# S5 coefficient generators on VectorE alone, in smaller steps, beside the first feed-forward layer

## The chip, the core and the metric

The kernel runs on one core of a Trainium2 chip. Five engines work side by side, each through its own instruction queue: TensorE (PE in the profile, with its weight loads shown as PEld), VectorE (DVE), ScalarE (ACT), GpSimd (POOL) and SyncE (SP), which here only issues transfers. ScalarE and GpSimd issue transfers too; the profile shows their issue slots as ACTq and POOLq. An instruction that waits holds up what stands behind it in its engine's queue. The metric is device time in microseconds (us), the median over several executions.

## The reference, cut to what matters

Two layers run over 1024 latent tokens and, in the first layer, 256 context tokens, with 1024 channels. Layer 0 mixes tokens by attention and retention, layer 1 by an S5 state-space scan in both directions; after each mixer comes a squared-ReLU feed-forward product ("MLP"). The change touches the preparation of the S5 scan's coefficients, which depends on parameters alone, and the place of some adaptive-modulation work in layer 1:

```
def s5_discretize(a_re, a_im, b_re, b_im, c_re, c_im, log_dt):
    a = lax.complex(f(a_re), f(a_im))
    dt = jnp.exp(f(log_dt))[:, None]
    a_bar = jnp.exp(dt * a)
    b_bar = ((a_bar - 1) / a)[..., None] * lax.complex(f(b_re), f(b_im))
    c_mat = lax.complex(f(c_re), f(c_im))
...
for l in range(DEPTH):
    mod_l = (silu(c) @ ada_w[l] + ada_b[l])       # six vectors of 1024
    h_l = modulate(rmsnorm(x, norm1_g[l]), mod_l[0], mod_l[1])
    o_l = mixer(h_l)                              # l = 0: attention and retention; l = 1: S5
    x = x + mod_l[2] * o_l
    h_l = modulate(rmsnorm(x, norm2_g[l]), mod_l[3], mod_l[4])
    x = x + mod_l[5] * (square(relu(h_l @ w1)) @ w2)
```

In layer 1 the mixer's output goes through a gated product: `z = gelu(y) @ w_glu`, then `za * sigmoid(zb)`.

## The kernel before

Every large product is done in three passes (`mm3`, lines 70 to 72): both operands are split into a high and a low part, and high-high, high-low and low-high are summed. For a weight tile `mraw` that SP has loaded, ScalarE makes the high part (`uh` or `dh`, line 76) and VectorE the low part (`ul` or `dl`, line 84). For the activations of the MLP's middle, ScalarE makes `r` (line 1053), `ah` (1056) and the square (1057), and GpSimd makes `al` (line 84). VectorE adds each finished bank of the second product to `x` (line 1070).

The first layer's MLP runs twice: first over 512 latent and 256 context tokens ("the first pass"), then over the other 512 latent tokens ("the second pass"). Each pass has 16 groups; a group does two blocks of the first product (`first`) and then the eight output tiles of the second product for the group before (`second`). In the first pass, from group 14 on, another generator (`last`, the normalisation of the second pass's tokens) takes the place of the side work.

Beside these passes runs one chain of Python generators, the side work: the modulation sums for layer 1 (`ada_rest`, tile `aw`, line 216), then the S5 generators in the order `s5_base`, `s5_outputs`, `s5_inputs`, `s5_tables`, and last the normalisation of two token blocks (`s5_in`, tile `us`). `beat` advances the chain by one step ("tick") each time a counter of matmul work, multiplied by a rate, passes one: a unit is one 512-column matmul, and the rate is `RA` = 0.07 in the first pass and `RB` = 0.125 in the second. `later(n, f)` emits f n ticks later. What the generators do:

- `s5_base` (lines 1144 to 1307): discretises and raises a_bar to powers 0 to 8 (`pw`) on 128x64 tiles, then makes `pb` (power times the factor (a_bar-1)/a, complex, for two directions) and `bb` (that factor times b). The real and imaginary parts of a complex product need two products and a sum each. One product of each pair is made by VectorE (lines 1271, 1298) and one by GpSimd (1272, 1299); VectorE sums them a tick later (1275, 1276, 1302, 1303). Twenty ticks after `pb`, TensorE transposes it and it is stored as `pbd`.
- `s5_outputs` (lines 1377 to 1420): 16 steps of two directions. In each, GpSimd makes four products of 128x288 elements (1402 to 1405, tile `oc`), VectorE joins them two ticks later (1408, 1409), ScalarE's queue stores them five ticks later (1414, `cst`), and `s5_lags` runs 32 small matmuls on them six ticks later (1433).
- `s5_inputs` (lines 1342 to 1375): 16 parts. SP loads two tiles `wb` (line 1350) and two `ww` (1353) of 256 KB for each part, one part ahead. For the real and the imaginary part GpSimd makes two products of 128x512 (1368, 1370, tile `wo`), VectorE sums them two ticks later (1371), and ScalarE's queue stores the sum five ticks after the second product (1373, `bst`).
- `s5_tables` (lines 1309 to 1340): cosine and sine tables, on VectorE and ScalarE.

All short-lived tiles of 512 elements come from one set of 32 buffers (`atile`); the MLP's split activations hold 16 of them.

After the second pass the S5 scan runs (`s5_main`), then the gated product (`glu`, from line 1564), two token halves `th` of eight output tiles `oc`; its side work is the modulation for the second layer's MLP, one step after every fourth matmul group (line 1586). The program text is not the order of execution in full: each engine has a queue order that was fixed when the program was built, and the trace shows side work standing ahead of or behind its place in the text.

Of the kernel before, what the change touches and what calls it, by code (L numbers as in the profile page):

```python
# [13 lines left out]
ALU = mybir.AluOpType  # L14
# [10 lines left out]
MAGIC = 12582912.0  # L25
NW = 14
RA = 0.07
RB = 0.125
BLOCKS = ((0, 512), (512, 512), (1024, 256))


# [20 lines left out]
class Net:  # L52
# [1091 lines left out]
    def s5_base(self):  # L1144
        nc, I = self.nc, self.I
# [119 lines left out]
        for d in range(2):  # L1265
            o, w = self.atile(name="pb"), self.atile(name="pbw")
            o4, w4 = (x.rearrange("p (s r q) -> p s r q", s=8, r=2) for x in (o, w))
            e = slice(0, 8) if d == 0 else slice(7, None, -1)
            bc = lambda K: K[:, d::2].unsqueeze(1).to_broadcast([P, 8, 32])
            for r in range(2):  # L1270
                tt(o4[:, :, r], pr[:, e, d::2], bc((kr, ki)[r]), ALU.mult)
                nc.gpsimd.tensor_tensor(w4[:, :, r], pi[:, e, d::2], bc((ki, kr)[r]), ALU.mult)

            def add(o4=o4, w4=w4):
                tt(o4[:, :, 0], o4[:, :, 0], w4[:, :, 0], ALU.subtract)
                tt(o4[:, :, 1], o4[:, :, 1], w4[:, :, 1], ALU.add)
            self.later(1, add)

            def turn(d=d, o=o):
                tp = self.bank()  # L1280
                for k4 in range(4):
                    nc.tensor.transpose(tp[:, k4 * P:(k4 + 1) * P], o[:, k4 * P:(k4 + 1) * P], self.ident)
                st = self.atile(name="pbs")
                nc.scalar.activation(st, tp, AF.Copy)
                nc.sync.dma_start(bass.AP(tensor=self.pbd.tensor, offset=self.pbd.offset + d * 65536,
                                          ap=[[P, P], [16384, 4], [1, P]]), st.rearrange("j (k n) -> j k n", k=4))
            self.later(20, turn)
            yield

        for d in range(2):  # L1290
            x, o, t = ([self.atile(name=nm) for _ in range(2)] for nm in ("b", "bb", "bt"))
            self.bb += [o]
            for r in range(2):
                nc.scalar.dma_start(x[r], I["s5b"][r, :, d])
            kb = lambda K: K[:, d::2].unsqueeze(2).to_broadcast([P, 32, 16])
            g3 = lambda x: x.rearrange("p (g h) -> p g h", h=16)
            for r in range(2):
                tt(g3(o[r]), g3(x[r]), kb(kr), ALU.mult)
                nc.gpsimd.tensor_tensor(g3(t[r]), g3(x[1 - r]), kb(ki), ALU.mult)

            def add(d=d, o=o, t=t):
                tt(o[0], o[0], t[0], ALU.subtract)
                tt(o[1], o[1], t[1], ALU.add)
                for r in range(2):
                    v.tensor_copy(self.bx[:, d, r, 0:16], o[r][:, 496:512])
            self.later(1, add)
            yield

    def s5_tables(self):

# [31 lines left out]
    def s5_inputs(self):  # L1342

        nc, I = self.nc, self.I
        parts = [(d, g0) for d in range(2) for g0 in range(0, 64, 8)]

        def fetch(d, g0):
            b, w = ([self.atile(name=nm) for _ in range(2)] for nm in ("wb", "ww"))
            for r in range(2):
                nc.sync.dma_start(b[r], bass.AP(  # L1350
                    tensor=I["s5bt"].tensor, offset=I["s5bt"].offset + (d * 2 + r) * 4096 + g0 * 64,
                    ap=[[0, 8], [16384, 16], [1, 512]]))
                nc.sync.dma_start(w[r], bass.AP(
                    tensor=self.pbd.tensor, offset=self.pbd.offset + (d * 16 + r) * 4096 + g0 * 64,
                    ap=[[8192, 8], [0, 16], [1, 512]]))
            return b, w
        gpv = lambda x: x.rearrange("p (q n) -> p q n", n=P)
        nx = fetch(*parts[0])
        for _ in range(4):
            yield  # L1360
        for k, (d, g0) in enumerate(parts):
            b, w = nx
            if k + 1 < len(parts):
                nx = fetch(*parts[k + 1])
            qs = slice(g0 // 2, g0 // 2 + 4)
            for r in range(2):
                x, t = (self.atile(name="wo") for _ in range(2))
                nc.gpsimd.tensor_tensor(x, w[0], b[r], ALU.mult)
                yield
                nc.gpsimd.tensor_tensor(t, w[1], b[1 - r], ALU.mult)  # L1370
                self.later(2, lambda r=r, x=x, t=t: nc.vector.tensor_tensor(
                    x, x, t, ALU.add if r else ALU.subtract))
                self.later(5, lambda qs=qs, d=d, r=r, x=x: nc.scalar.dma_start(self.bst[:, qs, d, r], gpv(x)))
                yield
                yield

    def s5_outputs(self, gp):

        nc, I = self.nc, self.I
        v = nc.vector  # L1380
        pr, pi = self.pw
        nc.scalar.dma_start(self.dr, I["s5d"])
        nc.scalar.dma_start(self.eye, I["eye16"])
        for it in range(16):
            qs = slice(2 * it, 2 * it + 2)
            if it % 4 == 0:
                c = self.atile(name="c5")
                nc.scalar.dma_start(c, I["s5c"][:, 8 * it // 4:8 * it // 4 + 8].rearrange("p q d r h -> p (q d r h)"))
                c = c.rearrange("p (q d r h) -> p q d r h", d=2, r=2, h=16)
            o1 = {}  # L1390
            for d in range(2):
                x = [c[:, 2 * (it % 4):2 * (it % 4) + 2, d, r] for r in range(2)]

                ks = slice(0, 9) if d == 0 else slice(8, None, -1)
                k0 = 1 if d == 0 else 0
                w = [pw[:, ks, 4 * it + d:4 * it + d + 3:2].rearrange("p k q -> p q k").unsqueeze(3).to_broadcast(
                    [P, 2, 9, 16]) for pw in (pr, pi)]
                xb = [a.unsqueeze(2).to_broadcast([P, 2, 9, 16]) for a in x]
                v9 = lambda t: t[:, :288].rearrange("p (q k h) -> p q k h", q=2, k=9)
                a, b, e, f = (self.atile(name="oc") for _ in range(4))  # L1400
                gp_tt = nc.gpsimd.tensor_tensor
                gp_tt(v9(a), xb[0], w[0], ALU.mult)
                gp_tt(v9(b), xb[1], w[1], ALU.mult)
                gp_tt(v9(e), xb[0], w[1], ALU.mult)
                gp_tt(v9(f), xb[1], w[0], ALU.mult)

                def join(a=a, b=b, e=e, f=f):
                    v.tensor_tensor(a[:, :288], a[:, :288], b[:, :288], ALU.subtract)
                    v.scalar_tensor_tensor(e[:, :288], e[:, :288], -1.0, f[:, :288], op0=ALU.mult, op1=ALU.subtract)
                self.later(2, join)  # L1410

                def store(qs=qs, d=d, a=a, e=e, k0=k0):
                    for r, t in enumerate((a, e)):
                        nc.scalar.dma_start(self.cst[:, qs, d, r], t[:, :288].rearrange("p (q k) -> p q k", q=2)[
                            :, :, 16 * k0:16 * k0 + P])
                self.later(5, store)
                o1[d] = [t[:, :288].rearrange("p (q k) -> p q k", q=2) for t in (a, e)]
                yield
            self.later(6, lambda it=it, o1=o1: self.s5_lags(it, o1))
            yield  # L1420

    def s5_lags(self, it, o1):
# [141 lines left out]
    def glu(self, p, x, after, side):  # L1564
# [3 lines left out]
        for th in range(2):  # L1568
# [9 lines left out]
            for oc in range(KT):  # L1578
                b = []
                for w in (oc + KT, oc):  # L1580
                    wt = self.split(p, I["glu"][w], "u")
                    z = self.bank()
                    for kt in range(KT):
                        self.mm3(z, wt(kt), yT[kt], kt == 0, kt == KT - 1)
                        if kt % 4 == 3:
                            next(side, None)
                    b.append(z)
                sgm = p.tile([P, 512], F32, tag="r", name="sgm", bufs=2)
                nc.scalar.activation(sgm, b[0], AF.Sigmoid)
                nc.vector.scalar_tensor_tensor(sgm, b[1], self.M[:, 1, 2, oc, 0:1], sgm, op0=ALU.mult, op1=ALU.mult)  # L1590
                xs = self.xh(x, oc, th)
                nc.gpsimd.tensor_tensor(xs, xs, sgm.rearrange("p (t c) -> p t c", t=4), ALU.add)  # L1592
                if th or oc:
                    after(*((th, oc - 1) if oc else (0, KT - 1)))
# [265 lines left out]
```

## Time and profile before

| what | value |
|---|---|
| median of 3 runs | 3227.12 us (3220.26 to 3232.1) |
| profiled execution, its own time | 3215.43 us |
| its span in the trace | 3213.6 us |
| granted TensorE clock, mean | 0.967 of full |
| TensorE busy | 92% of the span |
| VectorE, ScalarE, GpSimd busy | 66%, 38%, 29% |
| bytes moved, mean rate | 324.28 MB, 101 GB/s |

Durations and windows below come from the profiled execution. Its first MLP pass runs from about 1075 to 1665 us, the second from there to about 2082 us, the S5 scan to about 2285 us, the gated product to about 2500 us, and the second layer's MLP to the end. A window row of the profile gives, for a stretch of time, each engine's busy microseconds, with the number of instructions in brackets, then the granted TensorE clock, the share of the 16 DMA engines and the rate in GB/s. A row of the groups view gives line, engine, operation, tiles, shapes and count, then the total busy time and the mean of one in ns, then the engine's idle time just before them and what ended it. A timeline row gives start, duration, engine, line, tiles, and in square brackets the idle time before it and what ended it.

### The profile page before, as it was taken

How to read it: one execution, taken by the hardware profiler on the slowest of the kernel's cores; microseconds unless marked ns; L12 is line 12 of the kernel's file. 1: busy time of each engine (PE TensorE's matmuls, PEld its weight loads, DVE VectorE, ACT ScalarE, POOL GpSimd, SP SyncE). 2: the span in 40 equal slices, each digit the busy share in tenths (PEclk: the TensorE clock that was granted, in tenths of full speed). 3: DMA queues.
4: the chain of work that ended last, by engine and by line, in shares of the span. 5: the costliest groups of instructions: out<-in, count | busy, mean ns of one | idle time of the engine just before them, and what ended most of it. 6: DMA issues, size and time to landing. Idle time of an engine off the chain costs nothing. (4 is left out here: it accounts for less than half of the span.)

```text
span 3213.6 us, 45368 instructions
## 1 busy us (share of the span) xinstructions
PE 2968.0 (92%) x16683; PEld 2436.2 (76%) x16683; DVE 2111.0 (66%) x4014; ACT 1221.5 (38%) x2493; POOL 929.7 (29%) x902
## 2 busy tenths in 40 slices
PE   5899998899999998999997999967799999999998
PEld 3777777678878787887785778756678788888887
DVE  6777777687754688556468974378865555555555
ACT  6542222666762332222233664321334322222221
POOL 3642222455540113466326110123222111111111
PEclk8999999999999999999998999979999999999999
DMA  7132222301021452245426555287742111111111
GB/s 250 69 119 84 76 79 63 84 26 25 13 85 34 136 162 89 87 120 154 131 85 206 172 163 145 85 180 196 231 139 89 56 46 53 53 46 47 46 46 66
DMA packets 259039, 324.28 MB, mean 101 GB/s; under 512 B 72336, under 2 KB 179632, under 8 KB 258816
## 3 DMA queue, kind: packets, MB, share of 16 engines
q1 hardware_dynamic: 198352, 281.03, 29.0%
q10 hardware_dynamic: 59264, 36.84, 3.7%
q0 software_dynamic: 1200, 3.51, 0.4%
q8 instruction: 131, 2.15, 0.3%
q14 instruction: 92, 0.75, 0.1%
HBM read 267.96 MB, written 53.35 MB: 100 GB/s over the span
## 5 line engine op out<-in xcount | busy, mean ns | idle before, releaser
L84 POOL TENSOR_TENSOR al<-r,ah 128x512 fp32r<-128x512 f32 (+1 forms) x160 | 204.3, 1289 | 1191.5 <-ACT r L1057 1116.7
L1070 DVE SCALAR_TENSOR_TENSOR x<-b,mods,x 128x512 f32<-128x512 f32 (+1 forms) x483 | 457.5, 967 | 101.1 <-PE b L72 95.1
L84 DVE TENSOR_TENSOR ul<-mraw,uh 128x512 fp32r<-128x512 f32 x256 | 204.6, 803 | 429.3 <-ACT uh L76 428.7
L70 PE MATMUL b<-ah,dh 128*128 128x512 f32 (+1 forms) x1088 | 416.1, 383 | 21.4 <-ACT r L1053 10.2
L71 PE MATMUL b<-al,dh 128*128 128x512 f32 (+1 forms) x1088 | 413.7, 380 | 0.7 <-POOL al L84 0.7
L72 PE MATMUL b<-ah,dl 128*128 128x512 f32 (+1 forms) x1088 | 412.7, 380 | 0.5 <-DVE dl L84 0.4
L76 ACT ACTIVATE uh<-mraw 128x512 fp32r<-128x512 f32 x256 | 160.3, 628 | 453.3 <-PE b L71 261.3
L70 PE MATMUL b<-h2h,uh 128*128 128x512 f32 (+1 forms) x768 | 280.7, 366 | 21.8 <-DVE x L1070 11.6
L72 PE MATMUL b<-h2h,ul 128*128 128x512 f32 (+1 forms) x768 | 278.9, 364 | 18.6 <-DVE ul L84 18.4
L71 PE MATMUL b<-h2l,uh 128*128 128x512 f32 (+1 forms) x768 | 277.5, 361 | 0.0
L70 PEld LDWEIGHTS b<-ah,dh 128*128 128x128 f32 x1088 | 206.7, 190 | 64.8 <-DVE x L1070 11.6
L72 PEld LDWEIGHTS b<-ah,dl 128*128 128x128 f32 x1088 | 206.5, 190 | 40.5 <-DVE dl L84 1.9
L71 PEld LDWEIGHTS b<-al,dh 128*128 128x128 f32 x1088 | 207.0, 190 | 38.1 <-POOL al L84 1.1
L76 ACT ACTIVATE dh<-mraw 128x512 fp32r<-128x512 f32 x192 | 117.5, 627 | 248.2 <-PE b L71 119.6
L84 POOL TENSOR_TENSOR pl<-pe,ph 128x512 fp32r<-128x512 f32 (+1 forms) x128 | 158.3, 1246 | 154.9 <-ACT ph L76 86.8
L70 PE MATMUL b<-h3h,uh 128*128 128x512 f32 x512 | 202.0, 395 | 0.0
L71 PE MATMUL b<-h3l,uh 128*128 128x512 f32 x512 | 200.0, 391 | 2.0 <-DVE h3l L313 1.8
L72 PE MATMUL b<-h3h,ul 128*128 128x512 f32 x512 | 200.9, 393 | 0.0
L70 PEld LDWEIGHTS b<-h2h,uh 128*128 128x128 f32 x768 | 146.6, 191 | 50.5 <-DVE x L1070 14.2
L84 DVE TENSOR_TENSOR dl<-mraw,dh 128x512 fp32r<-128x512 f32 x192 | 150.5, 794 | 48.5 <-ACT dh L76 28.9
L72 PEld LDWEIGHTS b<-h2h,ul 128*128 128x128 f32 x768 | 146.4, 191 | 47.1 <-DVE ul L84 23.7
L1053 ACT ACTIVATE r<-b 128x512 f32<-128x512 f32 (+1 forms) x160 | 87.9, 550 | 244.9 <-PE b L72 170.8
(421 smaller groups left out, 7171.3 us busy)
## 6 DMA issues: line engine op xcount, KB each, us to landing
mraw<-in_w SPq DMA_DIRECT2D x192, 512.0 KB
aw<-in_adat SPq DMA_DIRECT2D x112, 256.0 KB
mraw<-in_glu SPq DMA_DIRECT2D x32, 512.0 KB
aw<-in_adat SPq DMA_DIRECT2D x96, 128.0 KB
CS<-csd SPq DMA_DIRECT2D x32, 320.0 KB
w<-in_adaw SPq DMA_DIRECT2D x32, 256.0 KB
wraw<-in_winr SPq DMA_DIRECT2D x32, 256.0 KB
cst<-oc ACTq DMA_DIRECT2D x64, 128.0 KB
```

The lines of the kernel that those rows point to most:

```text
L70: mm(o, s[0], m[0], start=start, stop=False)
L71: mm(o, s[0], m[1], start=False, stop=False)
L72: mm(o, s[1], m[0], start=False, stop=stop)
L76: self.nc.scalar.activation(o, x, AF.Copy)
L84: e.tensor_tensor(o, x, h.bitcast(F32), ALU.subtract)
L1053: nc.scalar.activation(r[:, :n], b[:, :n], AF.Relu)
L1070: nc.vector.scalar_tensor_tensor(o, as_x(b), self.M[:, l, 5, oc, s:s + 1], xs, op0=ALU.mult, op1=ALU.add)
```

## The change

The products that GpSimd made in `s5_base`, `s5_outputs` and `s5_inputs` are made by VectorE. In each generator the order becomes product, product, sum, directly one after the other or one tick apart, where the sums were deferred with `later`; the stores and `s5_lags` follow at the same or a shorter distance. `s5_base` and `s5_outputs` get more ticks, `s5_inputs` keeps its six per part. `RB` goes from 0.125 to 0.14. In the gated product the side steps of the first output tile (`th` = 0, `oc` = 0) are left out, so the modulation starts one tile later. `s5_tables`, `s5_lags` and all MLP code stay as they are.

```
-RB = 0.125
+RB = 0.14
...
             for r in range(2):
                 tt(o4[:, :, r], pr[:, e, d::2], bc((kr, ki)[r]), ALU.mult)
-                nc.gpsimd.tensor_tensor(w4[:, :, r], pi[:, e, d::2], bc((ki, kr)[r]), ALU.mult)
-
-            def add(o4=o4, w4=w4):
-                tt(o4[:, :, 0], o4[:, :, 0], w4[:, :, 0], ALU.subtract)
-                tt(o4[:, :, 1], o4[:, :, 1], w4[:, :, 1], ALU.add)
-            self.later(1, add)
+                yield
+                tt(w4[:, :, r], pi[:, e, d::2], bc((ki, kr)[r]), ALU.mult)
+                tt(o4[:, :, r], o4[:, :, r], w4[:, :, r], (ALU.subtract, ALU.add)[r])
+                yield
...
+            yield
+            yield
             for r in range(2):
                 tt(g3(o[r]), g3(x[r]), kb(kr), ALU.mult)
-                nc.gpsimd.tensor_tensor(g3(t[r]), g3(x[1 - r]), kb(ki), ALU.mult)
-
-            def add(d=d, o=o, t=t):
-                tt(o[0], o[0], t[0], ALU.subtract)
-                tt(o[1], o[1], t[1], ALU.add)
-                for r in range(2):
-                    v.tensor_copy(self.bx[:, d, r, 0:16], o[r][:, 496:512])
-            self.later(1, add)
-            yield
+                yield
+                tt(g3(t[r]), g3(x[1 - r]), kb(ki), ALU.mult)
+                yield
+                tt(o[r], o[r], t[r], (ALU.subtract, ALU.add)[r])
+                v.tensor_copy(self.bx[:, d, r, 0:16], o[r][:, 496:512])
+                yield
...
                 x, t = (self.atile(name="wo") for _ in range(2))
-                nc.gpsimd.tensor_tensor(x, w[0], b[r], ALU.mult)
+                nc.vector.tensor_tensor(x, w[0], b[r], ALU.mult)
                 yield
-                nc.gpsimd.tensor_tensor(t, w[1], b[1 - r], ALU.mult)
-                self.later(2, lambda r=r, x=x, t=t: nc.vector.tensor_tensor(
-                    x, x, t, ALU.add if r else ALU.subtract))
-                self.later(5, lambda qs=qs, d=d, r=r, x=x: nc.scalar.dma_start(self.bst[:, qs, d, r], gpv(x)))
+                nc.vector.tensor_tensor(t, w[1], b[1 - r], ALU.mult)
                 yield
+                nc.vector.tensor_tensor(x, x, t, ALU.add if r else ALU.subtract)
+                self.later(3, lambda qs=qs, d=d, r=r, x=x: nc.scalar.dma_start(self.bst[:, qs, d, r], gpv(x)))
                 yield
...
-                gp_tt = nc.gpsimd.tensor_tensor
-                gp_tt(v9(a), xb[0], w[0], ALU.mult)
-                gp_tt(v9(b), xb[1], w[1], ALU.mult)
-                gp_tt(v9(e), xb[0], w[1], ALU.mult)
-                gp_tt(v9(f), xb[1], w[0], ALU.mult)
-
-                def join(a=a, b=b, e=e, f=f):
-                    v.tensor_tensor(a[:, :288], a[:, :288], b[:, :288], ALU.subtract)
-                    v.scalar_tensor_tensor(e[:, :288], e[:, :288], -1.0, f[:, :288], op0=ALU.mult, op1=ALU.subtract)
-                self.later(2, join)
+                v.tensor_tensor(v9(a), xb[0], w[0], ALU.mult)
+                v.tensor_tensor(v9(b), xb[1], w[1], ALU.mult)
+                v.tensor_tensor(a[:, :288], a[:, :288], b[:, :288], ALU.subtract)
+                yield
+                v.tensor_tensor(v9(e), xb[0], w[1], ALU.mult)
+                v.tensor_tensor(v9(f), xb[1], w[0], ALU.mult)
+                v.scalar_tensor_tensor(e[:, :288], e[:, :288], -1.0, f[:, :288], op0=ALU.mult, op1=ALU.subtract)
...
-                self.later(5, store)
+                self.later(3, store)
...
-            self.later(6, lambda it=it, o1=o1: self.s5_lags(it, o1))
+            self.later(4, lambda it=it, o1=o1: self.s5_lags(it, o1))
...
-                        if kt % 4 == 3:
+                        if kt % 4 == 3 and (th or oc):
                             next(side, None)
```

## The prediction, written before the changed kernel ran

> **What bounds the kernel now.** First the page's table of busy time, then the windows of the two MLP passes beside which the generators run.
>
> ```profile
> PE 2968.0 (92%) x16683; PEld 2436.2 (76%) x16683; DVE 2111.0 (66%) x4014; ACT 1221.5 (38%) x2493; POOL 929.7 (29%) x902
> ```
> ```profile
> 1200.00:1280.00 80.00, 69.21 (x382) 59.07 (x381) 72.56 (x198) 19.60 (x41) 32.44 (x33) 0.96 0.28 86
> 1280.00:1360.00 80.00, 80.00 (x561) 69.04 (x560) 39.10 (x57) 22.84 (x49) 28.93 (x35) 1.00 0.30 91
> 1360.00:1480.00 120.00, 112.76 (x879) 93.22 (x878) 69.93 (x117) 34.94 (x82) 77.54 (x97) 1.00 0.39 115
> 1480.00:1560.00 80.00, 67.60 (x407) 57.29 (x406) 44.96 (x50) 18.41 (x40) 46.71 (x34) 0.91 0.64 201
> 1560.00:1640.00 80.00, 80.00 (x463) 70.41 (x462) 34.17 (x45) 25.96 (x52) 11.22 (x11) 1.00 0.22 67
> 1640.00:1760.00 120.00, 97.31 (x441) 77.55 (x440) 93.64 (x115) 38.27 (x66) 66.94 (x45) 0.86 0.54 169
> 1760.00:1880.00 120.00, 116.94 (x504) 93.98 (x503) 116.46 (x287) 78.67 (x140) 16.41 (x12) 1.00 0.58 176
> 1880.00:1960.00 80.00, 78.03 (x344) 63.83 (x344) 44.62 (x73) 45.42 (x76) 8.61 (x7) 0.98 0.56 148
> 1960.00:2040.00 80.00, 80.00 (x349) 65.04 (x348) 31.84 (x45) 32.16 (x52) 10.20 (x8) 1.00 0.40 122
> ```
>
> TensorE bounds the kernel, and only its idle time can be won. From 1200 to 1760 us it idles 10.79 + 0 + 7.24 + 12.40 + 0 + 22.69 = 53.1 us. The idle stretches are those with high POOL time; where GpSimd does nothing for the generators (1560 to 1640), PE is full. With VectorE at 116.46 of 120 us but GpSimd quiet (the tables, 1760 to 1880), PE still loses only 3.06 us. So a loaded VectorE alone is not what hurts.
>
> A gap also costs afterwards. After a gap of 6.26 us TensorE restarts at half clock:
>
> ```profile
> 1548.80:1552.80 4.00, 3.92 (x9) 3.15 (x10) 2.01 (x3) 0.03 (x1) 0.78 (x1) 0.50 1.02 283
> 1552.80:1556.80 4.00, 4.00 (x18) 3.26 (x17) 0.00 (x0) 0.15 (x1) 0.00 (x0) 0.90 0.55 194
> ```
>
> 9 matmuls in 4 us in place of 18: 2 us lost. The PE timeline shows six such slow starts, matmuls of 0.8 us behind a gap of over 3 us; the first and the last:
>
> ```profile
> 1253.26 0.80 PE L72 MATMUL b<-h2h,ul 128*128 128x512 f32 x1 [7.53 <-DVE ul L84]
> ...
> 1746.69 0.80 PE L70 MATMUL b<-h2h,uh 128*128 128x512 f32 x1 [8.49 <-DVE x L1070]
> ```
>
> One lies before 1280 us, two in 1480 to 1560, three after 1640: 12 us by these rows. The Trainium skill ("TensorE: Matmul & The Clock Gate", the HAM clock gate) puts the slow stretch at about 3.4 us at half clock; six of these would be an estimated 10 us, and the pool would shrink by 2. By the rows the pool is 53 + 12 = **65 us**, 2% of the time.
>
> Who keeps TensorE waiting: the waits of PE in 1200 to 1760, then the groups, and a stretch of the timeline of all engines.
>
> ```profile
> PE b L72 <- DVE ul L84: 18.4, 5, 7.5
> PE b L70 <- DVE x L1070: 16.7, 7, 8.5
> PE b L70 <- ACT r L1053: 10.2, 3, 6.3
> ```
> ```profile
> L84 DVE TENSOR_TENSOR dl<-mraw,dh 128x512 fp32r<-128x512 f32 x59 | 54.6, 947 | 17.3 <-ACT dh L76 17.3
> L1371 DVE TENSOR_TENSOR wo<-wo 128x512 f32<-128x512 f32 x32 | 40.2, 1258 | 18.6 <-POOL wo L1370 17.4 <-DMA wb<-in_s5bt 1.2
> L1408 DVE TENSOR_TENSOR oc<-oc 128x288 f32<-128x288 f32 x32 | 23.7, 741 | 21.6 <-POOL oc L1403 21.6
> L1409 DVE SCALAR_TENSOR_TENSOR oc<-oc 128x288 f32<-128x288 f32 x32 | 21.0, 657 | 25.1 <-POOL oc L1405 25.1
> ```
> ```profile
> 1722.64 1.77 DVE L1371 TENSOR_TENSOR wo<-wo 128x512 f32<-128x512 f32 x1 [1.19 <-POOL wo L1370]
> 1723.82 1.74 POOL L1370 TENSOR_TENSOR wo<-ww,wb 128x512 f32<-128x512 f32 x1
> 1724.44 0.37 ACTq L1373 DMA_DIRECT2D bst<-wo  x1
> 1724.85 0.63 ACT L1056 ACTIVATE ah<-r 128x512 fp32r<-128x512 f32 x1 [3.94 <-DVE wo L1371]
> ...
> 1725.59 1.76 DVE L1371 TENSOR_TENSOR wo<-wo 128x512 f32<-128x512 f32 x1 [1.18 <-POOL wo L1370]
> ```
>
> This is the mechanism. VectorE, in order, waits for GpSimd's product, 1.2 us each time. Its sum then takes 1.77 us, and GpSimd's next product is slow as well: the two slow each other. ScalarE's queue holds the store `bst`, which waits for that sum, and behind it stands `ah` of the MLP, idle for 3.94 us. VectorE's idle before sums is 17.4 + 21.6 + 25.1 = 64 us, all on POOL.
>
> **The change part by part.** The alone price of a VectorE operation:
>
> ```profile
> L1371 DVE TENSOR_TENSOR wo<-wo x32: 675/1334/1782, 1508.8 to 1751.6; 128x512 f32<-128x512 f32 x32
> L1298 DVE TENSOR_TENSOR bb<-b,gc x4: 679/685/1557, 1249.0 to 1254.3; 128x512 f32<-128x512 f32 x4
> L1409 DVE SCALAR_TENSOR_TENSOR oc<-oc x32: 445/459/1539, 1258.7 to 1481.0; 128x288 f32<-128x288 f32 x32
> ```
>
> The 512-element product costs 0.68 us, broadcast operand or not (1298 has one); the 288-element one 0.445. *Added to VectorE*: 64 products of `wo`, 43.5 us; 128 of `oc`, 57.0 us; the eight of `s5_base`, about 4 us; 105 us together. *Taken off it*: the slowing of sums, 32 x (1.258 - 0.68) + 32 x (0.741 - 0.445) + 32 x (0.657 - 0.445) = 34.8 us, and the 64 us of waits. The slowing of `ul` and `dl` I don't count, because GpSimd's `al` stays. Busy time in 1200 to 1760 was 354 of 560 us; plus 70 it would be 76% before any of it moves later.
>
> *Ticks.* From the loops: a first-pass group is 144 units, 10 ticks, the pass about 158 ticks. A second-pass group is 96 units: 12 ticks before, 13.44 at `RB` = 0.14. Steps of the chain: 270 before (41 modulation, 19 base, 48 outputs, 100 inputs, 44 tables, 18 normalisation), 324 after (41, 41, 80, 100, 44, 18). So base and outputs fill the first pass thinly, and all 16 parts of `s5_inputs` land in the second pass; before, 15 of their 32 pairs of products ran in one burst inside the first (its first and last rows below). A group of the second pass lasts 23.15 us (the two PE rows):
>
> ```profile
> 1501.50 1.26 POOL L1368 TENSOR_TENSOR wo<-ww,wb 128x512 f32<-128x512 f32 x1 [9.11 <-PE b L1433]
> ...
> 1548.32 1.26 POOL L1370 TENSOR_TENSOR wo<-ww,wb 128x512 f32<-128x512 f32 x1
> ...
> 1794.25 0.50 PE L70 MATMUL b<-h2h,uh 128*128 128x512 f32 x1 [0.76 <-DVE x L1070]
> 1817.40 0.50 PE L70 MATMUL b<-h2h,uh 128*128 128x512 f32 x1 [0.77 <-DVE x L1070]
> ```
>
> The side work of the second pass is then 324 - 162 = 162 ticks, 279 us. VectorE's own MLP share is 31.84 / 80 = 40% (the last window above), so 167 us are free. Wanted are 96 x 0.68 = 65 us of inputs, 116.46 - 0.4 x 120 = 68 of tables, 44.62 - 31.84 = 13 of normalisation: 146 us. VectorE runs at 92% there, but fits, and 373 - 324 = 49 ticks (84 us) are left before the pass ends, so the scan after it doesn't wait. If that cover went, each us of lag beyond 84 would be a us of time.
>
> *SP and the ScalarE queue.* The same loads and stores are issued; the store stands three ticks behind its sum as before, but the sum no longer hangs on GpSimd.
>
> *The gated product.* TensorE idles 11.22 us at its start, behind the modulation:
>
> ```profile
> 2270.95 21.32 SPq L212 DMA_DIRECT2D aw<-in_adat  x29
> 2292.32 1.37 SPq L1004 DMA_DIRECT2D mraw<-in_glu  x3
> 2298.48 0.90 PE L1573 MATMUL b<-ident,y 128*128 128x128 f32 x3 [11.22 <-DVE yl L84]
> ```
>
> 29 loads of `aw` go out before the first three weight loads, although the text has the first weight load ahead of them. So the queue order does not follow the text closely, and beginning the side steps a tile later may move nothing: 0 at one end, 11.2 us at the other. I take 2, near the no-move end, since the loads are already 20 us ahead of their place.
>
> *The sum*, idle time and slow starts of each stretch against what I leave, by choice near the 3.06 us per 120 of the tables' window: 1200 to 1280, 10.8 + 2, left 4: -9. 1360 to 1480, 7.2, left 3: -4. 1480 to 1560, 12.4 + 4, its inputs gone, left 3: -13. 1640 to 1760, 22.7 + 6, left 14 (4 for 160 us more of a full VectorE at that rate, 10 for loads and queues that come late): -15. Gated product -2. Together **-43 us**: 3172 from the profiled execution's 3215.43, and 3227.12 - 43 = 3184 from the median, which I predict; the profiled execution lies 12 us under the median, and the difference is carried over.
>
> **The rivals.**
>
> *More than that*: nearly all 65 us go, 3 at the tables too, and up to 11 at the gated product: -60 to -79, 3148 to 3167. For it: windows without GpSimd work lose nothing. Against: `ul` and `r` also wait for late loads.
>
> *No gain*: the gaps come from side work standing too early in the queues, whoever does it; VectorE then blocks as GpSimd did, within 16 us of 3227. For it: the queue order above. Against: the 64 us of VectorE waiting on POOL, which has no successor.
>
> *Slower: VectorE waits for loads.* The products now stand in VectorE's queue in front of `ul`, `dl` and `x`, so a late `ww` or `wb` stops these too; GpSimd took such waits before. A part is 6 ticks, 10.3 us; VectorE's slack in it is 0.6 x 10.3 - 6 x 0.68 = 2.1 us. If each of 16 parts finds its loads D late, TensorE loses 16 x (D - 2.1); that eats up the gain of 43 and the 14 already left at D = 5.7. If the whole latency shows, as of the 256 KB load in the last row here (7.2 us from issue to landing),
>
> ```profile
> mraw<-in_w SPq DMA_DIRECT2D x192, 512.0 KB
> ...
> wb<-in_s5bt SPq DMA_DIRECT2D x32, 256.0 KB
> ...
> bst<-wo ACTq DMA_DIRECT2D x32, 256.0 KB
> ...
> silr<-in_crow POOLq DMA_DIRECT2D x8, 256.0 KB, 7.2
> ```
>
> it is 16 x 5.1 - 57 = +25: 3252. Against: loads run a part ahead, and 1.0 MB of loads, 0.5 of stores and 0.9 of weights (four `mraw` a group) per 10.3 us are 237 GB/s, under the 283 seen above. The Trainium skill ("Perfetto Trace Analysis", Optimizing Scalar/DVE Operations) says that offloading from a saturated VectorE, even to GpSimd, may make sense; by that rule the move is wrong where VectorE is at 92%. It adds that the two share a port, so that such a move might not help; the slow pairs at 1722 us agree with that.
>
> **How the numbers follow.** Forecast case (-20 to -62, 3165 to 3207) 0.56; more 0.15; no gain 0.16; slower 0.13. About 0.5%, 16 us, is what a measurement can tell from no change here. Faster: 0.56 + 0.15 = 0.71; same 0.16; slower 0.13. The range reaches from 3148, the end of the larger gain, through no gain to 3240, half of the slower case: 3148 to 3240.
>
> **What would show it.** Right: in the windows of the first pass PE within 2 or 3 us of full; no slow starts there; `oc` sums near 0.45 us; VectorE's waits on POOL gone; all `wo` after about 1640. In the second pass VectorE above 85% to about 1950, PE losing 10 to 15 us. Wrong: VectorE idle before `wo` on DMA by tens of us; `ul` or `x` as PE's releaser in the second pass beyond 20 us; the scan's first load waiting for `us`; the 11 us gap at the gated product gone entirely, or more.

## The result and the profile after

The changed kernel takes 3205.9 us in the median of 10 runs (3198.56 to 3218.11), the kernel before 3224.93 us in 10 runs on the same chip (3212.52 to 3232.1). The ratio is **0.9947, interval 0.993 to 0.9964**: 0.53% faster, less than half of the 43 us that were forecast. The profiled execution of the changed kernel took 3218.11 us (span 3216.3), 12 above its median, while that of before lay 10 below the median of its ten. The two whole spans (3213.6 and 3216.3 us) therefore say little: ahead of the first MLP pass, where nothing was changed, the traced execution of after took 16 us more (the pass begins at 1075.09 us before and at 1091.44 after; in the runs below anywhere from 1071 to 1091). The comparison goes by stages, each from one execution; by their sum the change gains 14 us, by the medians 19.

The page's table of busy time, the kernel after:

```profile
PE 2983.0 (93%) x16683; PEld 2456.6 (76%) x16683; DVE 2144.8 (67%) x4214; ACT 1221.6 (38%) x2493; POOL 730.3 (23%) x702
```

GpSimd lost 200 instructions and 199 us; VectorE gained 200 instructions and only 34 us. In the two passes the sums of inputs and outputs take 29 us less than before, and `ul` and `dl`, whose slowing the prediction did not count, 19 us less. The windows of the two passes, the kernel after, in the bounds that the prediction used:

```profile
1200.00:1280.00 80.00, 75.75 (x413) 65.32 (x412) 74.12 (x225) 21.38 (x43) 9.62 (x8) 0.98 0.35 111
1280.00:1360.00 80.00, 80.00 (x464) 70.53 (x464) 34.27 (x45) 23.98 (x48) 9.46 (x10) 1.00 0.20 61
1360.00:1480.00 120.00, 120.00 (x822) 104.71 (x821) 74.97 (x142) 39.25 (x82) 19.51 (x14) 1.00 0.34 102
1480.00:1560.00 80.00, 80.00 (x549) 68.84 (x548) 54.86 (x108) 22.96 (x50) 10.73 (x8) 1.00 0.34 101
1560.00:1640.00 80.00, 80.00 (x569) 69.58 (x568) 50.69 (x93) 26.18 (x54) 8.85 (x8) 1.00 0.28 84
1640.00:1760.00 120.00, 106.68 (x552) 85.70 (x550) 88.53 (x150) 41.86 (x78) 13.00 (x10) 0.96 0.61 183
1760.00:1880.00 120.00, 107.20 (x432) 86.30 (x433) 95.10 (x178) 48.82 (x83) 11.96 (x9) 0.91 0.67 210
1880.00:1960.00 80.00, 76.11 (x323) 61.06 (x322) 79.23 (x203) 49.97 (x88) 9.95 (x7) 0.98 0.57 177
1960.00:2040.00 80.00, 69.43 (x285) 55.73 (x284) 43.25 (x78) 44.40 (x76) 6.45 (x5) 0.91 0.67 164
```

From 1280 to 1640 PE is full. But from 1760 to 2040, where it lost 5 us before, it now loses 12.8 + 3.9 + 10.6 = 27 us. For an exact account each pass is taken as one window, between three marks of the PE timeline: its first matmul `b<-h2h,uh`, the 256-column `z<-al,dh` of the first pass's last group that waits 0.45 us for `al`, and the first `b<-ones,sqa` behind the second pass. The kernel before:

```profile
1075.09:1667.07 591.98, 560.09 (x3520) 479.57 (x3520) 382.30 (x722) 181.53 (x378) 216.87 (x226) 0.98 0.39 121
1667.07:2082.26 415.19, 386.31 (x1650) 309.93 (x1650) 289.42 (x521) 196.87 (x335) 110.57 (x77) 0.95 0.52 155
```

The kernel after:

```profile
1091.44:1644.50 553.06, 547.39 (x3424) 475.33 (x3424) 383.05 (x815) 181.46 (x372) 76.52 (x64) 0.99 0.33 103
1644.50:2084.82 440.32, 398.58 (x1746) 320.23 (x1746) 321.44 (x628) 197.39 (x342) 52.19 (x39) 0.95 0.61 179
```

The first pass is **38.9 us shorter**, the second **25.1 us longer**, and the rest (to the end of the span) takes 1131.5 us against 1131.3. Idle time of PE fell by 26.2 in the first pass (31.9 to 5.7) and rose by 12.9 in the second (28.9 to 41.7). The remainder is in the busy column: 96 small matmuls of `s5_lags` moved from one pass into the other (about 5 us: e5 and e8 below, with 1746 and 1649 matmuls in this pass at a clock of 0.99, are busy 384 and 379 us), and the slow starts after gaps moved with the gaps.

Who keeps PE waiting in the second pass (1640 to 2085), the kernel after; a row of the waits view gives who waits for whom, the us in total, how often, and the longest:

```profile
PE b L70 <- DVE x L1070: 25.8, 8, 5.8
PE b L70 <- ACT uh L76: 5.1, 2, 2.7
```

In the kernel before, PE's wait for `x` in this window was 12.6 us. The sum `x` itself is never long, at most 0.75 us here. A stretch of the timeline, the kernel after, shows what it stands behind:

```profile
1691.63 0.60 SPq L1347 DMA_DIRECT2D wb<-in_s5bt  x1
...
1692.97 0.57 SPq L1350 DMA_DIRECT2D ww<-pbd  x1
...
1694.78 0.33 SPq L1004 DMA_DIRECT2D mraw<-in_w  x1
...
1704.38 0.63 ACT L76 ACTIVATE uh<-mraw 128x512 fp32r<-128x512 f32 x1 [10.57 <-DMA mraw<-in_w]
...
1705.04 0.69 DVE L84 TENSOR_TENSOR ul<-mraw,uh 128x512 fp32r<-128x512 f32 x1 [4.53 <-ACT uh L76]
1705.65 0.74 DVE L1070 SCALAR_TENSOR_TENSOR x<-b,mods,x 128x512 f32<-128x512 f32 x1
...
1706.45 0.80 PE L70 MATMUL b<-h2h,uh 128*128 128x512 f32 x1 [5.02 <-DVE x L1070]
```

The weight tile is used 9.6 us after its load was issued. `uh` is late, VectorE's `ul` waits for it, `x` stands behind `ul`, and PE waits for the bank that `x` empties; then it restarts with a matmul of 0.80 us. The chain runs from a load through two in-order queues to PE. ScalarE's waits in the second pass, the kernel after, have the weight load at their head:

```profile
ACT uh L76 <- DMA mraw<-in_w: 46.8, 12, 10.6
```

The same row in the second pass of the kernel before (1667 to 2083):

```profile
ACT uh L76 <- DMA mraw<-in_w: 23.5, 13, 3.9
```

So ScalarE waited for weights before, too, and as often, but not as long (the one long wait, 8.3 us, stood before a `dh`).

### The profile page after: what moved, and what is told of

Read it like the earlier page. It is cut to its first block, busy times and chain, and to the rows that moved or that the text cites. A ratio compares the mean times of both kernels' runs of the same rounds, so it can differ in the third digit from the quotient of the medians.

```text
span 3216.3 us, 45163 instructions
## 1 busy us (share of the span) xinstructions
PE 2983.0 (93%) x16683; PEld 2456.6 (76%) x16683; DVE 2144.8 (67%) x4214; ACT 1221.6 (38%) x2493; POOL 730.3 (23%) x702
## 5 line engine op out<-in xcount | busy, mean ns | idle before, releaser
L84 DVE TENSOR_TENSOR ul<-mraw,uh 128x512 fp32r<-128x512 f32 x256 | 195.8, 772 | 394.2 <-ACT uh L76 393.4
L70 PEld LDWEIGHTS b<-h2h,uh 128*128 128x128 f32 x768 | 149.0, 194 | 67.0 <-DVE x L1070 28.2
L70 PE MATMUL z<-wh,hh 128*128 128x512 f32 (+1 forms) x400 | 163.2, 408 | 13.0 <-ACT scr L497 7.2
```

The source lines that it names most:

```text
L70: mm(o, s[0], m[0], start=start, stop=False)
L84: e.tensor_tensor(o, x, h.bitcast(F32), ALU.subtract)
```

## The experiments

Ratios are to the kernel before on the same chip; stages are in us, between the marks above, each from the profiled execution.

| kernel | first pass | second | rest | ratio, interval |
|---|---|---|---|---|
| before | 592.0 | 415.2 | 1131.3 | 1 |
| after | 553.1 | 440.3 | 1131.5 | 0.9947 (0.993 to 0.9964) |
| e1_ra10 | 566.0 | 410.9 | 1127.3 | 0.9893 (0.9878 to 0.9909) |
| e2_halfload | 552.5 | 407.5 | 1135.3 | 0.9859 (0.9841 to 0.9877) |
| e3_poolstore | 552.7 | 448.1 | 1129.6 | 0.9958 (0.9938 to 0.9978) |
| e4_oneop | 552.1 | 447.1 | 1129.7 | 0.9971 (0.9955 to 0.9988) |
| e5_halfbytes | 552.4 | 400.5 | 1136.1 | 0.9845 (0.9817 to 0.9873) |
| e6_engineonly | 565.4 | 408.6 | 1127.3 | 0.992 (0.9899 to 0.9941) |
| e7_ra12 | 582.4 | 416.5 | 1134.1 | 0.9971 (0.9954 to 0.9988) |
| e8_ra10rb11 | 566.2 | 393.2 | 1132.2 | 0.9856 (0.9833 to 0.9879) |
| e9_rb11 | 553.5 | 410.6 | 1137.4 | 0.9878 (0.985 to 0.9906) |
| e10_engrb09 | 564.0 | 394.8 | 1126.4 | 0.9856 (0.9832 to 0.988) |
| e11_gluback | 552.8 | 441.2 | 1131.3 | 0.9957 (0.9938 to 0.9977) |
| e12_befrb09 | 592.9 | 413.0 | 1129.9 | 0.9988 (0.997 to 1.0006) |
| e13_mraw4 | 553.8 | 423.7 | 1131.9 | 0.9919 (0.9895 to 0.9942) |
| e14_poolload | 553.0 | 413.5 | 1132.8 | 0.989 (0.9869 to 0.9911) |
| e15_mraw4_rates | 565.7 | 393.3 | 1133.8 | 0.9865 (0.9846 to 0.9884) |
| e16_poolload_rates | 573.7 | 393.0 | 1135.4 | 0.9864 (0.9833 to 0.9896) |

### What lengthens the second pass: transfers, VectorE's work, or stores in ScalarE's queue

Theory A: the parts' transfers crowd out the weight loads. B: VectorE has too much to do. C: ScalarE's queue is held by the stores. e1, the changed kernel at a higher rate, begins the parts in the first pass again:

```
-RA = 0.07
+RA = 0.10
```

> The changed kernel with RA = 0.10 in place of 0.07: the side work runs faster in the first MLP pass, so about ten of the 16 parts of the inputs generator fall into it and six into the second pass. In the changed kernel's trace the first pass lasts 553 us (before 592) and the second 440 us (before 415). Theory A (the loads of all 16 parts crowd the transfers of the second pass, and weights come late): second pass falls to 400 to 415 us, the first rises by less than 15, net 10 to 30 us faster than the changed kernel. Theory B (VectorE has too much work in the second pass): the same direction, second pass to 400 to 415 us, and VectorE's backlog at the end of the pass goes. Theory C (ScalarE's queue is held by the stores of the inputs): the loss goes along with the parts, so the first pass gains what the second loses, net within 10 us of the changed kernel.

e2 loads the two `wb` tiles for the first part alone:

```
+        one = [self.atile(name="wb") for _ in range(2)]
...
-            b, w = ([self.atile(name=nm) for _ in range(2)] for nm in ("wb", "ww"))
+            b, w = one, [self.atile(name="ww") for _ in range(2)]
...
-                nc.sync.dma_start(b[r], bass.AP(
+                if d + g0 == 0:
+                    nc.sync.dma_start(b[r], bass.AP(
```

> The changed kernel with the two b tiles of the inputs generator loaded for the first part alone and used for all 16 (the later parts' coefficients are left out): half of the generator's loads are gone, 8 MB of 16, while VectorE's work and the stores stay. Theory A (crowded transfers): second pass from 440 down to 410 us or less, ScalarE's wait for weight loads in it from 47 us to under 25. Theory B (VectorE's work): second pass within 8 us of 440. Theory C (stores in ScalarE's queue): within 8 us of 440.

e3 issues the stores elsewhere:

```
-                self.later(3, lambda qs=qs, d=d, r=r, x=x: nc.scalar.dma_start(self.bst[:, qs, d, r], gpv(x)))
+                self.later(3, lambda qs=qs, d=d, r=r, x=x: nc.gpsimd.dma_start(self.bst[:, qs, d, r], gpv(x)))
```

> The changed kernel with the 32 stores of the inputs generator issued from GpSimd's queue in place of ScalarE's. Theory C (ScalarE held by stores that wait for sums; ScalarE waits 48 us for wo sums in the second pass): second pass from 440 to 415 us or less, and those waits go. Theories A and B: second pass within 8 us of 440, since loads and VectorE's work stay.

e4 keeps all transfers and a third of VectorE's operations in `s5_inputs`:

```
...
-                nc.vector.tensor_tensor(x, w[0], b[r], ALU.mult)
+                nc.vector.tensor_tensor(x, w[r], b[r], ALU.mult)
                 yield
-                nc.vector.tensor_tensor(t, w[1], b[1 - r], ALU.mult)
                 yield
-                nc.vector.tensor_tensor(x, x, t, ALU.add if r else ALU.subtract)
```

> The changed kernel with one product in place of product, product, sum for each half of a part of the inputs generator (two of three VectorE operations are left out, 64 of 0.69 us or 44 us; loads, stores and ticks stay). Theory B (VectorE's work): second pass from 440 to 415 us or less. Theory A (crowded transfers): within 8 us of 440. Theory C (stores waiting for sums): between, since the store hangs on one operation less, 425 to 440 us.

In e1 the parts begin at 1494 us, and the second pass falls to 410.9 us while the first grows to 566.0; about 5 us of each is the 96 small matmuls, which go back to the first pass. With two thirds of the inputs' VectorE work gone (e4) the second pass is 447 us, no shorter than after's 440; VectorE's waits for `ww` grow to 44.3 us, so the time set free goes into waiting for loads. With the stores out of ScalarE's queue (e3) the pass is 448 us, and PE waits only 0.5 us for `al`, so GpSimd, which now holds the stores, isn't what costs. With half of the loads gone (e2) it is 407.5, and ScalarE's wait for `mraw` falls to 28.2 us, not quite under the 25 expected. VectorE's load and the stores in ScalarE's queue fall as causes of the 25 us; the loads stay.

e2 took away bytes and issues together. e5 keeps number and order of the loads and halves their bytes:

```
-                nc.sync.dma_start(b[r], bass.AP(
+                nc.sync.dma_start(b[r][:, 0:256], bass.AP(
...
-                    ap=[[8192, 8], [0, 16], [1, 512]]))
+                    ap=[[8192, 8], [0, 16], [1, 256]]))
```

> The changed kernel with every load of the inputs generator cut to its first 256 columns, and the products reading those columns twice (half of each coefficient tile is not the reference's): as many loads, in the same queue order, with half the bytes; VectorE's work and the stores stay. With half the loads left out altogether the second pass fell by 32 us. Theory A1 (the bytes on the DMA engines delay the weights): second pass again 20 to 35 us shorter than the changed kernel's 440. Theory A2 (not the bytes but the number of loads ahead of the weight loads in SP's queue, each waiting for its buffer): within 10 us of 440.

The second pass came to 400.5 us, 40 shorter and so beyond theory A1's 20 to 35: it is the bytes and not the count of issues. ScalarE's waits in e5's second pass (1636 to 2037):

```profile
ACT uh L76 <- DMA mraw<-in_w: 22.9, 11, 5.4
```

Half of after's 46.8 us, and the longest wait 5.4 in place of 10.6.

### Which edit costs it

e6 is the kernel before with nothing but its products on VectorE; the steps, the deferred sums and RB = 0.125 stay:

```
...
-                nc.gpsimd.tensor_tensor(x, w[0], b[r], ALU.mult)
+                nc.vector.tensor_tensor(x, w[0], b[r], ALU.mult)
...
-                gp_tt = nc.gpsimd.tensor_tensor
+                gp_tt = v.tensor_tensor
```

> The kernel before with one edit: the products of the three generators run on VectorE, at their old places; ticks, deferred sums and stores, RB and the gated product as before. Half of the inputs' parts then stay in the first pass. Theory A (the change's gain is the engine, its loss is that the finer steps push all 16 parts into the second pass): first pass 560 to 575 us against 592 before, second pass 385 to 410 against 415 before, 30 to 50 us faster than before. Rival (VectorE alone is the loss): second pass 430 us or more, no faster than the changed kernel. Rival (the finer steps are what freed the first pass): first pass within 10 us of 592.

The engine move alone gives 0.992 (the medians differ by 31 us, the low end of the 30 to 50 expected): 26.6 us in the first pass and 6.6 in the second. The rest of the change, finer steps and RB = 0.14, wins another 12.3 in the first, where no part is left, and costs 31.7 in the second, where all 16 are (about 5 us of either is the 96 small matmuls).

### How the rates act

e7 and e8 are the changed kernel with other rates:

```
-RA = 0.07
+RA = 0.12
```

> The changed kernel with RA = 0.12: all 16 parts of the inputs generator fall into the first pass by the count of ticks (270 ticks, of which they need up to 262), where a group's weights are spread over 34 us in place of 23. Theory A: second pass 385 to 395 us, first pass at most 25 us longer than 553, so as good as RA = 0.10 or better by up to 10 us. If the first pass has too little room for all parts: first pass 590 us or more, and no gain over RA = 0.10.

```
-RA = 0.07
-RB = 0.14
+RA = 0.10
+RB = 0.11
```

> The changed kernel with RA = 0.10 and RB = 0.11: the steps left for the second pass (98) are spread over 169 ticks in place of 215, so that loads, tables and normalisation come further apart. Theory A: second pass 5 to 15 us shorter than with RA = 0.10 and RB = 0.14, first pass the same. If the pace in the second pass no longer matters once half of the parts are gone: within 5 us.

e7 missed both expectations: with nearly all parts in the first pass that pass takes 582 us, 29 more than after, so part of the loss moves with the parts. But the second pass, almost without parts, still takes 416.5 us, no better than with RA = 0.10. A window of it, in which the tables run:

```profile
1700.00:1760.00 60.00, 51.07 (x213) 39.06 (x212) 60.00 (x165) 40.38 (x74) 7.47 (x5) 0.98 0.60 178
```

VectorE is never idle there, and PE loses 8.9 us, more than half of it behind `dl` and `ul`. This points to VectorE's own work, in the tables at this pace; no run separates it. e8, with the parts across both passes and a slower second pass, beats both kernels at 0.9856; its second pass is 18 us shorter than e1's, a little more than the 5 to 15 expected.

e9 changes only RB in the changed kernel:

```
-RB = 0.14
+RB = 0.11
```

> The changed kernel with RB = 0.11 in place of 0.14, RA left at 0.07. All 16 parts of s5_inputs still fall into the second pass, spread over 22% more time. Theory A (bytes of the parts beside the weight loads): the first pass stays at 551 to 555 us, the second comes down from 440 to 412 to 428, the ratio to the kernel before is 0.986 to 0.992. Rival (only where the parts stand counts, not how densely): the second pass stays at 433 to 447 and the ratio at 0.993 to 0.997. If the side work is no longer done at the second pass's end, the stage after it is over 1140 us.

e10 is e6, and e12 the kernel before, each with this one line changed:

```
-RB = 0.125
+RB = 0.09
```

> The kernel before with its products on VectorE (steps, deferred sums and stores as before) and RB = 0.09 in place of 0.125. Theory A: the first pass stays at 564 to 567 us, as with the engine alone; the second, which was 409, comes to 395 to 403; the ratio is 0.986 to 0.990. If pace no longer counts once part of the inputs lies in the first pass: the second pass stays at 406 to 411 and the ratio at 0.991 to 0.993. If the side work then ends late: the stage after the second pass is over 1140 us.

> The kernel before with nothing changed but RB = 0.09 in place of 0.125: products stay on GpSimd, and the second pass's share of the side work is spread over 39% more time. Theory A (the second pass loses by transfers crowding beside the weight loads, whoever multiplies): the first pass stays at 590 to 594 us, the second comes from 415 to 398 to 408, the ratio is 0.993 to 0.998. Rival (with the products on GpSimd the second pass is bound by VectorE and GpSimd waiting for each other, so pace moves nothing): second pass 411 to 418, ratio 0.998 to 1.002. Side work ending late would show as over 1140 us after the second pass.

In e9 and e10 the second pass came out a little better than theory A expected (410.6 and 394.8), but in e9 not by its reason. `wo` of e9, by tile (min, median and max in ns, then first and last start in us):

```profile
L1365 DVE TENSOR_TENSOR wo<-ww,wb x32: 676/684/692, 1683.3 to 1831.6; 128x512 f32<-128x512 f32 x32
```

The same line of the kernel after:

```profile
L1365 DVE TENSOR_TENSOR wo<-ww,wb x32: 678/686/693, 1684.0 to 1840.4; 128x512 f32<-128x512 f32 x32
```

The 16 parts take 148 us against 156: they were not spread. The window 1700 to 1800 of e9 even moves more:

```profile
1700.00:1800.00 100.00, 87.75 (x358) 70.38 (x357) 66.97 (x106) 31.36 (x54) 10.83 (x8) 0.93 0.77 242
```

The same window of the kernel after:

```profile
1700.00:1800.00 100.00, 80.32 (x314) 64.00 (x313) 65.78 (x103) 27.76 (x48) 8.15 (x6) 0.90 0.70 219
```

and of e5, with PE nearly full at after's own rate:

```profile
1700.00:1800.00 100.00, 98.92 (x429) 79.99 (x428) 92.73 (x147) 38.00 (x65) 13.43 (x9) 1.00 0.71 219
```

A rate of 219 GB/s goes with a PE at 80 and with one at 99. Theory A in its simple form, so many bytes per us crowd out the weights, falls. In e12, the kernel before, pace alone gives nothing (0.9988, second pass 413.0), as the rival expected and not theory A. Its two longest gaps stand behind `ul` and `x` (6.51 and 9.04 us), as they do in the kernel before, with the products on GpSimd.

e9 also paid 6 us behind the second pass: its side work ends late, and the scan's first matmul has waited 20.79 us for `ut<-ud`, against 14.29 in e8.

### Lead, queue, or the DMA engines

e13 gives the changed kernel a fourth weight tile; e14 takes the parts' loads out of SP's queue; e15 is e8 with e13's edit, and e16 e8 with e14's.

```
-        w = p.tile([P, 1024], F32, tag="raw", name="mraw", bufs=3)
+        w = p.tile([P, 1024], F32, tag="raw", name="mraw", bufs=4)
```

> The changed kernel with four tiles mraw in place of three, so that a weight load can be issued one tile earlier; bytes, queues and rates as in the changed kernel. Too short a lead: the second pass comes from 440 to 400 to 420 us, ScalarE's wait for mraw before uh in it from 46.8 us to under 25, the ratio is 0.983 to 0.990. Engines that carry no more: the second pass stays at 433 to 447, the wait above 40, the ratio at 0.993 to 0.997. First pass 550 to 554 in both.

```
-                nc.sync.dma_start(b[r], bass.AP(
+                nc.gpsimd.dma_start(b[r], bass.AP(
...
-                nc.sync.dma_start(w[r], bass.AP(
+                nc.gpsimd.dma_start(w[r], bass.AP(
```

> The changed kernel with the loads of wb and ww issued from GpSimd's queue in place of SyncE's; bytes, lead and rates as in the changed kernel. Weights standing behind the parts' loads in SyncE's queue: the second pass comes to 400 to 420 us and the ratio to 0.983 to 0.991. Engines that carry no more, or too short a lead: the second pass stays at 433 to 450 and the ratio at 0.993 to 0.999. If GpSimd's issuing holds up its own al, TensorE waits for al by more than 5 us.

> The changed kernel with four tiles mraw, RA = 0.10 and RB = 0.11. Lead counts wherever the parts are loaded: the first pass comes from 566 to 555 to 562, the second from 393 to 385 to 391, the ratio to 0.978 to 0.984. Lead no longer counts once the parts are spread over both passes: 564 to 567, 391 to 396, ratio 0.984 to 0.987.

> The changed kernel with the loads of wb and ww in GpSimd's queue, RA = 0.10 and RB = 0.11. SyncE's queue costs there too: the first pass comes from 566 to 554 to 561 us, the second from 393 to 385 to 391, the ratio from 0.986 to 0.978 to 0.984. The bytes alone, or GpSimd's issuing costs what the queue gains: first pass 563 to 568, second 391 to 398, ratio 0.984 to 0.988.

In e13 ScalarE's wait for `mraw` falls to 17.5 us as expected, but the pass only to 423.7, just outside the range. Its VectorE waits (1660 to 1830) show what came in place:

```profile
DVE wo L1367 <- DMA ww<-pbd: 13.2, 6, 2.7
...
DVE wo L1367 <- DMA bst<-wo: 7.9, 2, 4.4
DVE wo L1365 <- DMA ww<-pbd: 6.4, 6, 1.8
DVE wo L1365 <- DMA bst<-wo: 2.4, 1, 2.4
```

With the weights earlier, the parts' loads are late: 30 us, of which the kernel after had 16. The timeline of e13 has the chain of the prediction's slower rival, a product waiting for `ww` with `x` behind it:

```profile
1712.11 0.69 DVE L1367 TENSOR_TENSOR wo<-ww,wb 128x512 f32<-128x512 f32 x1 [2.14 <-DMA ww<-pbd]
1712.72 0.69 DVE L1365 TENSOR_TENSOR wo<-ww,wb 128x512 f32<-128x512 f32 x1
1713.32 0.75 DVE L1070 SCALAR_TENSOR_TENSOR x<-b,mods,x 128x512 f32<-128x512 f32 x1
```

In e14 those waits of VectorE on DMA are 3.2 us, PE's waits for `x` 15.0 in place of 25.8, and the pass 413.5. Its window 1700 to 1800:

```profile
1700.00:1800.00 100.00, 93.14 (x389) 74.69 (x388) 84.29 (x125) 33.00 (x57) 35.94 (x50) 0.97 0.98 265
```

The engines carry 265 GB/s, so they were not at their limit at 219. What held them was the one queue, in which weights and parts stand behind each other and behind buffers. The DMA queue's own waits (1684 to 1846), SP in the kernel after, show it standing for transfers of the parts:

```profile
SPq L1004 <- DVE dl L84: 48.6, 11, 9.0
...
SPq L1347 <- DMA bst<-wo: 11.3, 5, 4.5
SPq L1350 <- DMA bst<-wo: 9.0, 3, 6.0
SPq L1347 <- DMA wb<-in_s5bt: 4.8, 3, 2.1
SPq L1350 <- DMA wb<-in_s5bt: 4.0, 4, 1.3
```

In the first row a weight load waits for its own tile to come free; in the others a part's load waits for a store or an earlier load of the parts, and the weight loads behind it wait too. Over all rows SP's queue waits 40 us for transfers of the parts; in e14, in the same window, 1.8 us. The Trainium skill ("DMA: Bandwidth & Descriptors", Queues, rings and completion order) says that within one queue each DMA engine takes descriptors in order, which fits a weight tile landing late behind four loads of a part. The same page (Issuing engines are not separate DMA queues) says that a second issuing engine saves only issue time, which is usually small. Here it raised 219 to 265 GB/s and took 27 us off the pass, while the first queue's waiting for parts went: more than issue time was saved, and the measurement decides.

How the shorter queue reaches PE is not shown in full. ScalarE's waits in e14 (1620 to 2060):

```profile
ACT uh L76 <- DMA mraw<-in_w: 49.0, 12, 6.8
```

Their sum is no smaller than after's 46.8; only the longest fell. In the nine runs with all 16 parts in the second pass the longest wait goes with the pass where the sum does not: 9.2 to 13.4 us in after, e3, e4 and e11 (440 to 448 us), 4.6 to 7.1 us in e2, e5, e9, e13 and e14 (400 to 424 us). PE's longest gap behind `x` fell in e14 from 5.8 to 2.6 us.

Where many of the parts lie in the first pass neither cure helps: e15 gives 0.9865, e16 0.9864, against 0.9856 of e8. In e16 the first pass even grows to 573.7, which neither expectation held. Of the 13 us that the first pass takes longer with parts in it (e8's 566.2 against 553.1), 7 are busy time of PE, mainly the 96 small matmuls; what the other 6, idle time, come from, these runs leave open.

### The gated product

e11 undoes the edit in `glu`:

```
-                        if kt % 4 == 3 and (th or oc):
+                        if kt % 4 == 3:
```

> The changed kernel with the edit in the gated product undone (a side step after every fourth matmul group of the first tile too). Forecast's choice, 2 us by the edit: the stage from the second pass's end to the end of the kernel grows from 1131.5 to about 1133.5. No move: it stays at 1130 to 1133 and the ratio at 0.993 to 0.997, with TensorE idle 9 to 11.5 us at the start of the gated product in both. If the edit were worth the whole gap: about 1142 us and a ratio near 0.998.

The rest is 1131.3 us against 1131.5: the edit moves nothing. In the kernel after, PE still idles at that place:

```profile
2298.50 1.97 PE L1566 MATMUL b<-ident,y 128*128 128x128 f32 x8 [9.74 <-DVE yl L84]
```

and 29 loads of `aw` are still issued ahead of the first three weight loads:

```profile
2272.95 20.70 SPq L212 DMA_DIRECT2D aw<-in_adat  x29
2293.71 1.37 SPq L1004 DMA_DIRECT2D mraw<-in_glu  x3
```

## Why the prediction was right or wrong

**Right: the mechanism of the first pass.** The pairs of VectorE and GpSimd were the main loss: VectorE's waits on POOL before these sums are gone, PE is full from 1280 to 1640, and e6 shows the engine move alone giving 26.6 us there. I had forecast 26 in the first pass, but for the whole change, so that the two figures agree is chance; the whole change gave 38.9, since I left 10 us of loss in stretches that lost 4.25, and since work and slow starts left the pass as well. The prices held: 0.686 us for the large product against 0.68, 0.45 against 0.445 for the small one. So did the ticks: every `wo` starts at 1684 us or later. (Of the 32 pairs of products, 13 and not 15 ran in the first pass before.)

**Wrong: the second pass's term**, "1640 to 1760 ... -15", of which "10 for loads and queues that come late". The second pass became 25 us longer. The window to 1760 itself came out near the 14 that I left in it, with 13.3 us of idle time and two slow starts. But the sum ended at 1760, although my own ticks had moved the inputs of the first pass, and with them the tables and the normalisation, into 1760 to 2085. For that stretch I entered only the 4 us of "160 us more of a full VectorE"; it lost 27 us of idle time to 2040, against 5 before. So the forecast -43 is, by stages, -38.9 in the first pass, +25.1 in the second and nothing in the gated product.

**The argument that let this pass** was "237 GB/s, under the 283 seen": it compared a mean rate with a peak. What counts is whether a weight tile lands before ScalarE needs it, and in the timeline at 1694 us that hung on what stood ahead of it in SP's queue; e5 and the kernel after have the same rate and 99 and 80 us of PE. e2, e5 and e14 show that the parts' loads in this queue cost the time.

**VectorE at 92%** was wrong, and harmless in this kernel. Over 1640 to 1880 it was busy 184 of 240 us; in the tables' window, at 79.23 of 80 us, PE lost 3.9; and e4 took work off it for no gain. That "a loaded VectorE alone is not what hurts" may not hold at every pace, though, as the window of e7 above suggests. The Trainium skill's rule that I cited ("Perfetto Trace Analysis", Optimizing Scalar/DVE Operations), that offloading a saturated VectorE, even to GpSimd, may make sense, did not bear on this kernel: VectorE was busy 66% of the span before, and e6 moved the work the other way and gained 0.8%.

**The slower rival** had the right kind of place, a queue in order behind a late load, on the wrong engine. VectorE waited for parts 16 us in all (1660 to 1830); ScalarE waited for weights 46.8 us. Only in e13, with the weights earlier, were VectorE's waits for parts the larger of the two (30 against 17.5 us). Of the signs that I named as wrong, one came: `x` as PE's releaser beyond 20 us.

**The gated product**: 2 us forecast, nothing measured; the row with 29 loads of `aw` in front had said so.

**Open**: why a lower RB helps although the parts aren't spread (e9), and how SP's queue and ScalarE's waits add up to the pass (e14). Not all of the idle time stands beside the parts: they end at 1846 us, and of the 10.6 us that PE idles in 1960 to 2040 the PE timeline puts 5.5 behind `acc` and `rsc` of the normalisation, 2.8 behind `uh`, which waits for a weight tile, and 1.6 behind `dl`. What moved these waits into PE's way isn't shown.

## What to carry to other kernels

When an edit moves side work to a later stage, carry the sum to the end of that stage and enter the work's loads there, not only its engine time. Price a late load by what stands ahead of it in its own queue and by the time from issue to use of the tile behind it; a mean rate below a peak excuses nothing. Moving work to the engine that adds its results paid here (e6). Cutting it finer isn't shown to pay: with lower rates the finer steps reach 0.9856 (e8), and so does the engine move alone with RB = 0.09 (e10).

## What the runs showed of the hardware

In 1700 to 1800 us one core moved 219 GB/s, at a DMA share of 0.70, with parts and weights in one queue, and 265 GB/s, at 0.98, with the parts' loads issued by GpSimd. The length of a gap alone did not decide whether TensorE restarted slowly: behind one of 2.37 us (after, 1945.6 to 1948.6) the granted clock was 0.50, behind one of 3.06 us (before, 1367.2 to 1369.2) it was 1.00. GpSimd's issue of a store took longer than ScalarE's. `bst` by tile, e3:

```profile
L1370 POOL DMA_DIRECT2D bst<-wo x32: 750/752/804, 1669.0 to 1829.6; - x32
```

and the kernel after:

```profile
L1370 ACTq DMA_DIRECT2D bst<-wo x32: 366/366/377, 1688.5 to 1846.5; - x32
```
